# Float32 products in units, HGRN corners with 32-column weights, and a changed order of projections in a planned one-core encoder layer

## The chip, the cores and the metric

The kernel runs on one core of one Trainium2 chip. The metric is device time in microseconds of one execution; "the time" is the median of several. A profiled execution has its own time, and a span from its first instruction to its last. The engines are named as in the profile: PE is TensorE's matmuls and PEld its weight loads, DVE is VectorE, ACT is ScalarE, POOL is GpSimd, SP is SyncE, which issues the DMAs.

## The reference

One layer is applied to two sequences, a prompt of 512 tokens and a sample of 1024 tokens, with a model width of 1024:

```python
h = rms_norm(x, n_pre_mix)
proj = h @ w_in            # split: qkv, z, a, b, q_h, f_h, i_h, g_h, gate_raw
# bidirectional gated delta rule, 4 heads of 128, chunks; q, k, v behind a 5-tap conv and silu
o_a = gated_delta_chunked(q, k, v, g[0], beta[0]) + flip_seq(gated_delta_chunked(...flipped...))
y_a = (rms_norm(o_a, gdn_norm_w) * silu(z_g)) @ w_br_gdn
# bidirectional HGRN2, 4 heads of 128: f = lb + (1 - lb) * sigmoid(f_h), k = 1 - f
o_b = gla_chunked(qh, kh[0], ih, logf[0]) + flip_seq(gla_chunked(...flipped...))
y_b = (rms_norm(o_b, hg_norm_w) * silu(g_h)) @ w_br_hg
merged = gates[:, :, 0] * y_a + gates[:, :, 1] * y_b
x = x + rms_norm(merged @ w_out, n_post_mix)
h2 = rms_norm(x, n_pre_ffn)
ff = (silu(h2 @ w_gate) * (h2 @ w_up)) @ w_down
return x + rms_norm(ff, n_post_ffn)
```

Everything is float32. The chunked forms above are one way to compute the two recurrences; the kernel uses chunks of 128 tokens.

## The kernel before, in words

**Two kinds of matmul.** The large products (projections, branches, the dense part) split each float32 operand into a high and a low part in a reduced format (F32R) and add three matmuls (`mm3`). Each moves 512 columns over 128x128 weights, and a projection of 128 output columns over one block of 512 tokens is 8 x 3 = 24 of them. Its weights are loaded by one DMA (`in_w`, `get_w`) and split by ScalarE (`AF.Copy`) and VectorE (a subtraction). The small products of the mixer are float32 itself: 128x128x128 in the recurrences and for Gram matrices, transpositions against an identity, and products on 64x64, 32x32 or 128x32 parts of the array. In the trace a float32 product is two matmul records, and a transposition is one.

**The order of work is written by a program.** The function `layer` doesn't issue instructions. It records them on a `Tape`, in an order that `Plan.run` makes from five streams (`gdn_stream`, `hg_stream`, `pre_stream`, `dense_stream`, `p2_stream`). Each stream yields where it waits, for a time or for marks of other streams (`need`, `pl.mark`). Among the streams that are ready the first in the list goes on. Then `Tape.schedule` places the recorded instructions with a model of costs (`cost`: `occ` is how long the engine is taken, `dur` how long the result takes). It looks up to `AHEAD` = 500 instructions past the oldest one that hasn't been placed, and takes, on the engine that is free first, the ready instruction that stands earliest in the record. What comes out is one fixed list per engine.

**Forms and units.** A product whose weights aren't 128x128 has a `form` (rows, columns of its weights). `units` puts neighbouring products of one form, with no other matmul in between in the record, no dependence among them by way of another engine, and at most two fresh banks of PSUM, in one unit. A unit is placed as a whole, when all that its members wait for is there. The model adds `SWITCH` = 400 ns when the form changes. Float32 products with 128x128 weights and transpositions have no form before: each is placed alone, between F32R matmuls as it comes.

**HGRN corners** (`hg_attn`). Per head and block of 512 tokens, the attention inside chunks of 128 tokens is put together from levels. The 64-level, the corners of each chunk, is a product of `l64` with itself for each direction `d` and chunk `t`: 128 columns of weights, of which 64 rows of the result are needed, by 64 columns. Then come 48 products with 32-column weights, the diagonal blocks (`e2`, `e1`) and the 32-level (`l32`), each on one of four column strips of the array.

**GDN recurrence** (`gdn_mix`). Per head and chunk of 128 tokens, both directions take a step: a product with the state (`pks`), one with the inverse's factor (`pr_`), one for the new state (`pu`), with VectorE operations between, and two for the output (`po`).

**The dense list** (`dense`, `dense_stream`). For each head, projections are listed with what they wait for: z, q, i, the two forget gates f, and g. For the first sequence z and g wait for the HGRN output of the head before (`zk`), and q, i, f for that of two heads before (`hk`). `pick` takes the first item of this list if what it waits for is there, else the first open one of the 16 projections of output gates (`gates`), some of which are held back until a head's inverse or end.

**The norm of the second sequence** (`pre_stream`, `prelude`) begins when `("gin", 0)` is marked, in the last head of the first sequence, behind its inverse. It loads rows of `x_sample`, scales them, transposes them on TensorE and splits them. Its second block waits for the end of the first sequence's dense list.

Of the kernel before, what the change touches and what calls it, by code (L numbers as in the profile page):

```python
# [20 lines left out]
P = 128  # L21
# [18 lines left out]
WBUFS = (2, 2, 2)  # L40
HOLD = ((3, 2, 1, 2), (2, 2, 2, 2))
MSTEP = (24, 28)
CPOS = 3
QSQ = P * EPS ** 0.5
EPSQ = P * EPS * EPS
# [2 lines left out]
class Op:  # L48

    __slots__ = ("idx", "eng", "meth", "args", "kw", "occ", "dur", "tiles", "need", "succ", "rel", "prio", "form", "unit",  # L50
                 "asked", "port")


class VT:
# [100 lines left out]
class Tape:  # L155
# [5 lines left out]
    TAIL = {"ACT": 95, "DVE": 75, "POOL": 40}  # L161
    LANES = 8
    SWITCH = 400
    AHEAD = 500
    RATE = 260.0
    SLACK = {"sync": 600, "vector": 100, "scalar": 100, "gpsimd": 100, "tensor": 100}
# [12 lines left out]
    def __init__(self, nc):  # L179
        self.nc = nc  # L180
        self.fake = bacc.Bacc("TRN2", target_bir_lowering=False, num_devices=1)
        for n in self.ENGS:
            setattr(self, n, Tape.Eng(self, n))
        self.ops = []
        self.vts = {}
        self.pools = {}
        self.masks = {}
        self.cuts = {}
        self.count = 0

    def cut(self, name):

# [67 lines left out]
    def cost(self, o, out, ins, scal):  # L260
        e, m = o.eng, o.meth
        n = self.free_size(out)

        def psum(a):
            v = self.vts.get(a.tensor.name)
            return v is not None and v.pool.kind == "PSUM"
        if m == "dma_start":
            vo = self.vts.get(out.tensor.name)
            run = self.row(out, ins[0])
            rows = out.shape[0] * n // run  # L270
            o.form = rows * max(run * 4, 512) / self.RATE
            if vo is None or vo.pool.kind == "DRAM":
                o.dur = 1200.0
            elif [x for x in ins[0].ap if x[0] == 0 and x[1] > 1]:
                o.dur = 4000.0
            else:
                o.dur = 2000.0
            o.occ = 380.0 if rows < 512 else 450.0
            if o.dur < 2000.0 and run < P:
                o.occ = 600.0  # L280
            return
        if e == "tensor":
            if m == "transpose":
                o.occ = 110
            else:
                k = self.free_size(ins[1])
                form = (ins[0].shape[0], self.free_size(ins[0]))
                if ins[1].dtype == F32R:
                    o.occ = k / 2.4 + 13.5
                else:  # L290
                    o.occ = 2 * (2 * k / 2.4 + 5.5) if k > 32 else 24
                    if form != (P, P):
                        o.form = form
                        if form == (64, 64):
                            o.occ = 62
            o.dur = o.occ + 165
            return
        if e == "scalar":
            d = 200 + 0.84 * self.free_size(ins[0]) - (45 if psum(ins[0]) else 0) + 92 * len(scal)
            o.dur, o.occ = d, d - (95 if o.kw.get("accum_out") is None else 0)  # L300
            return
        if e == "vector":
            ps = psum(out) or any(psum(i) for i in ins)
            if not ps and m != "memset" and (m != "tensor_scalar" or n > 1):
                o.port = 138 + 65 * len(scal)
            if m == "tensor_tensor_scan":
                d = 155 + 1.98 * n
            elif m in ("tensor_copy", "tensor_scalar", "memset") and not ps:
                d = 145 + 0.53 * n
            else:  # L310
                d = 145 + 1.055 * n
            if m in ("copy_predicated", "transpose"):
                d += 30
            d += 65 * len(scal)
            o.dur, o.occ = d, d - 75
            return
        if m == "memset":
            d = 90 + 0.86 * n
        elif m == "affine_select":
            d = 100 + 1.05 * n  # L320
        else:
            d = 192 + (1.87 if n < TB else 2.15) * n
        if m != "memset":
            o.port = 138
        o.dur, o.occ = d, d - 40

    def add(self, eng, meth, args, kw):
        o = Op()
        o.idx = o.prio = len(self.ops)
        o.eng, o.meth, o.args, o.kw = eng, meth, args, kw  # L330
        o.form, o.unit, o.port = None, [o], 0
        out = args[0]
        ins = [a for a in args[1:] if isinstance(a, bass.AP)]
        scal = []
# [49 lines left out]
    def units(self):  # L384


        cur, taint, fresh = None, set(), set()
        for o in self.ops:
            if o.eng == "tensor" and o.form is not None:
                new = {v for v in o.tiles if v.pool.kind == "PSUM" and v.ops[0] is o}  # L390
                if cur and cur[0].form == o.form and not any(j in taint for j in o.need) and len(fresh | new) <= 2:
                    cur.append(o)
                    o.unit = cur
                else:
                    cur, taint, fresh = [o], set(), set()
                    o.unit = cur
                fresh |= new
            elif o.eng == "tensor":
                cur = None
            elif cur and any(j in taint or self.ops[j].unit is cur for j in o.need):  # L400
                taint.add(o.idx)

    def schedule(self):
# [77 lines left out]
        while done < len(ops):  # L481
# [18 lines left out]
            while fu and fu[0][0] <= t:  # L500
                i = heapq.heappop(fu)[1]
                heapq.heappush(re_, (ops[i].prio, i))
            o = ops[heapq.heappop(re_)[1]]
            w = t
            for x in o.unit:
                for v in x.tiles:
# [12 lines left out]
                lanes.append(t + o.dur)  # L519
            if e == "tensor":  # L520
                if o.form is not None and o.form != form:
                    t += self.SWITCH
                form = o.form
            if o.port:
                w = max(0.0, held["gpsimd" if e == "vector" else "vector"] - t - o.port)
# [186 lines left out]
def layer(ctx, tc, x_p, x_s, w_in, conv_w, a_log, dt_bias, gdn_w, lb_logits, hg_w, w_bg, w_bh,  # L712
# [631 lines left out]
    def gdn_mix(q, h, gi):  # L1344
# [125 lines left out]
        zn = []  # L1470
        for step in range(nt):
            pos, rrs = [], []
            for d in range(2):
                tg = step if d == 0 else nt - 1 - step
                b, t = divmod(tg, 4)
                tsl = slice(t * P, (t + 1) * P)
                pos.append((d, tg, b, t, tsl))
                if step == 0:
                    rrs.append(vtok[b][:, tsl])
                else:  # L1480
                    rr = sblk("rr")
                    pks = px()
                    mm(pks[:, 0:P], kT[b][:, tsl], st[d])
                    stt(rr, pks[:, 0:P], q.nec[:, tg, d, h:h + 1], vtok[b][:, tsl], ALU.mult, ALU.add)
                    rrs.append(rr)
            if step:
                yield None
            raws, vks = [], []
            for d, tg, b, t, tsl in pos:
                pr_ = px()  # L1490
                mm(pr_[:, 0:P], ws[b, d][:, t, :], rrs[d])
                if step < nt - 1:
                    vk = sblk("vk")
                    ts(vk, pr_[:, 0:P], vcs[b, d][:, t:t + 1], ALU.mult)
                    vks.append(vk)
                raw_ = sblk("raw_")
                copy(raw_, pr_[:, 0:P])
                raws.append(raw_)
            yield None
            new = {}  # L1500
            for d, tg, b, t, tsl in pos:
                if step < nt - 1:
                    pu = px()
# [4 lines left out]
                    else:  # L1508
                        stt(sn, st[d], ers[b, d][:, t:t + 1], pu[:, 0:P], ALU.mult, ALU.add)
                    new[d] = sn  # L1510
            for d, tg, b, t, tsl in pos:
                if step % 4 == 0:
                    po[d] = px()
                if step > 0:
                    mm(po[d][:, tsl], st[d], qd[b, d][:, tsl], True, False)
                mm(po[d][:, tsl], raws[d], at[b, d][:, tsl], step == 0, True)
            st = new
            for d, tg, b, t, tsl in pos:
                if step % 4 == 3:
# [3 lines left out]
                    else:  # L1523
                        tt(oT[b], oT[b], po[d], ALU.add)
                        zn.append(b)
            yield None
        yield need(("z", q.si, h))
        for b in zn:
            yield from out_norm(q, oT[b], g_gdn, q.z["z", h][b], h, b, gi["q2"][b])

    def dense(q):
        for h in range(HEADS):
# [33 lines left out]
            zk = hgk(h - 1)  # L1566
            hk = hgk(h - 1 if q.si else h - 2)
            dep = ("h", q.si, 0)
            yield (zk, dep, ("gdn", 0, 3) if q.si else dep), C_Z + h * P, zcb(("z", h)), ("z", q.si, h)
            yield (hk, dep), C_QH + h * P, cbq, None  # L1570
            yield (hk, dep), C_IH + h * P, cbv, None
            yield (hk, dep), C_FH + h * P, cbf(0), None
            yield (hk, dep), C_FH + 512 + h * P, cbf(1), ("hgin", q.si, h)
            yield (zk, ("gdn", q.si, h) if q.si else dep), C_GH + h * P, zcb(("G", h)), ("G", q.si, h)

    def gates(q):
# [57 lines left out]
    def hg_attn(q, h):  # L1634
        out = q.hg[h]
        for b in range(q.nb):
# [4 lines left out]
            pav, pbv = t4(pa), pb[:, 0:P].rearrange("p (t c) -> p t c", c=32)  # L1641
            halves = [slice(0, 64), slice(64, P)]
            yield pl.at(parts[0]["l64"], parts[1]["l64"], parts[0]["l32"], parts[1]["l32"])
            for d in range(2):
                dl = t4(parts[d]["l64"])
                for t in range(4):
                    mm(pav[:, t, halves[1 - d]], dl[:, t, :], dl[:, t, halves[1 - d]])
            for d in range(2):
                e1, e2, l32 = [parts[d][n] for n in ("e1", "e2", "l32")]
                for t in range(4):  # L1650
# [350 lines left out]

    def pre_stream():
        yield from prelude(seqs[0])
        yield need(("gin", 0))
        yield from prelude(seqs[1])

    def gdn_stream():
# [321 lines left out]
```

## Time and profile before

| what | value |
|---|---|
| median of 3 runs | 2482.34 us (2479.26 to 2483.96) |
| profiled execution, its own time | 2481.04 us |
| its span | 2479.3 us |
| mean granted TensorE clock | 0.995 |
| busy PE, PEld | 2437.4 us (98%), 2018.0 us (81%) |
| busy DVE, ACT, POOL | 1708.0 us (69%), 1276.8 us (51%), 730.7 us (29%) |
| matmul records | 13968 |
| moved by DMA | 330.37 MB, mean 133 GB/s |

The mixer takes the first half of the span, up to about 1200 us; the branches, the output projection and the dense part take the rest. Busy time of PE counts from a matmul's start to its modelled end, and matmuls overlap, so the distance from one start to the next is the better price of one. Every emitted instruction has the line of `emit`, 596, so the profile tells them apart by tiles and shapes. The tiles are large areas: `ha_a` holds the normed inputs, `wa_a` the split weights, `la_a`, `ba_a` and `sm_a` the mixer's blocks, `sa_a` constants such as the identity, and `bank` is PSUM.

### The profile page before, as it was taken

The page shows a single profiled execution, that of the slowest core. Times are in us where ns is not written, and L with a number is a line of the kernel's source. Part 1 is how long each engine was busy: PE and PEld are TensorE (multiplying, and loading weights), DVE is VectorE, ACT ScalarE, POOL GpSimd, SP SyncE. Part 2 cuts the span into 40 slices and gives each one's busy share as a digit, 9 for nine tenths or more (in the row PEclk, how much of TensorE's full clock was granted, in tenths as well). Part 3 has the DMA queues.
Part 4 walks back from the last instruction along what each step waited for, and adds up shares of the span by engine and source line. Part 5 has one row for each costly group of instructions (what it writes and reads, how often), then busy time and mean ns, then how long its engine had stood idle before and what let it go on. Part 6 is the DMA issues. An engine that isn't in the chain of part 4 may idle for free. (4 is left out here: it accounts for less than half of the span.)

```text
span 2479.3 us, 37545 instructions
## 1 busy us (share of the span) xinstructions
PE 2437.4 (98%) x13968; PEld 2018.0 (81%) x13968; DVE 1708.0 (69%) x2843; ACT 1276.8 (51%) x2166; POOL 730.7 (29%) x1011
## 2 busy tenths in 40 slices
PE   7999999999999999999999999999999999999998
PEld 6878887888888888888888888788888888888886
DVE  6868779758867677677747754664788777635458
ACT  5756667646646646546544543543444434433342
POOL 1541504141333232321000002123567675200014
PEclk9999999999999999999999999999999999999999
DMA  6234453322340330332747624544355455584463
GB/s 163 75 87 128 105 148 98 108 51 62 90 103 31 94 95 30 92 93 68 265 155 272 217 84 128 157 147 125 126 178 183 157 181 169 183 274 133 153 205 114
DMA packets 387302, 330.37 MB, mean 133 GB/s; under 512 B 55241, under 2 KB 315935, under 8 KB 387119
## 3 DMA queue, kind: packets, MB, share of 16 engines
q1 hardware_dynamic: 387119, 327.97, 43.5%
q8 instruction: 110, 1.80, 0.3%
q14 instruction: 73, 0.60, 0.1%
HBM read 251.44 MB, written 76.46 MB: 132 GB/s over the span
## 5 line engine op out<-in xcount | busy, mean ns | idle before, releaser
L596 PE MATMUL bank<-ha_a,wa_a 128*128 128x512 f32 x5496 | 1452.4, 404 | 5.8 <-ACT ha_a L596 2.3
L596 PEld LDWEIGHTS bank<-ha_a,wa_a 128*128 128x128 f32 x5496 | 1005.2, 189 | 194.2 <-DVE wa_a L596 7.6
L596 PE MATMUL bank<-xr_a,ha_a 128*128 128x512 f32 x1200 | 319.3, 395 | 0.0
L596 PE MATMUL bank<-xr_a 128*128 128x512 f32 x1386 | 315.2, 389 | 0.0
L596 PEld LDWEIGHTS bank<-xr_a 128*128 128x128 f32 x1386 | 260.1, 188 | 54.1
L596 PEld LDWEIGHTS bank<-xr_a,ha_a 128*128 128x128 f32 x1200 | 225.4, 188 | 53.9
L596 POOL TENSOR_TENSOR ba_a<-ba_a 128x512 f32<-128x512 f32 (+1 forms) x125 | 176.7, 1420 | 241.2 <-DVE ba_a L596 94.3
L596 ACT ACTIVATE la_a<-la_a 128x512 f32<-128x512 f32 (+1 forms) x335 | 209.6, 644 | 55.8 <-DVE la_a L596 42.0
L596 DVE TENSOR_TENSOR wa_a<-la_a,wa_a 128x1024 fp32r<-128x1024 f32 (+1 forms) x140 | 161.9, 1167 | 93.3 <-PE bank L596 68.9
L596 ACT ACTIVATE wa_a<-la_a 128x1024 fp32r<-128x1024 f32 (+1 forms) x140 | 136.3, 982 | 130.5 <-PE bank L596 125.3
L596 ACT ACTIVATE wa_a<-ba_a 128x1024 fp32r<-128x1024 f32 (+1 forms) x106 | 99.6, 950 | 137.8 <-PE bank L596 117.9
L596 DVE TENSOR_TENSOR wa_a<-ba_a,wa_a 128x1024 fp32r<-128x1024 f32 (+1 forms) x106 | 119.8, 1135 | 56.8 <-PE bank L596 43.1
L596 ACT ACTIVATE ha_a<-ba_a 128x512 fp32r<-128x512 f32 x130 | 81.3, 629 | 142.7 <-PE bank L596 95.4
L596 PE MATMUL bank<-ha_a 128*128 128x512 f32 x480 | 149.4, 392 | 0.0
L596 DVE TENSOR_TENSOR ha_a<-ba_a,ha_a 128x512 fp32r<-128x512 f32 x130 | 125.5, 968 | 18.9 <-ACT ha_a L596 18.6
L596 PE MATMUL bank<-wa_a,ha_a 128*128 128x512 f32 x576 | 134.1, 390 | 1.6 <-DVE wa_a L596 1.6
L596 DVE TENSOR_TENSOR la_a<-la_a 128x512 f32<-128x512 f32 (+2 forms) x184 | 125.0, 693 | 10.4 <-ACT la_a L596 9.6
L596 PEld LDWEIGHTS bank<-wa_a,ha_a 128*128 128x128 f32 x576 | 108.0, 188 | 24.5 <-DVE wa_a L596 2.0
L596 DVE TENSOR_TENSOR xr_a<-da_a,xr_a 128x1024 fp32r<-128x1024 f32 (+2 forms) x66 | 76.7, 1174 | 68.2 <-ACT xr_a L596 46.1
L596 ACT ACTIVATE xr_a<-da_a 128x1024 fp32r<-128x1024 f32 (+2 forms) x66 | 64.5, 993 | 114.7 <-PE bank L596 114.1
L596 PEld LDWEIGHTS bank<-la_a 128*32 128x32 f32 (+3 forms) x1836 | 102.5, 130 | 20.0 <-issue 4.6
L596 PE MATMUL bank<-la_a 128*32 128x32 f32 (+4 forms) x1836 | 107.7, 216 | 2.0 <-DVE la_a L596 1.6
(192 smaller groups left out, 3452.2 us busy)
## 6 DMA issues: line engine op xcount, KB each, us to landing
la_a<-w_in SPq DMA_DIRECT2D x77, 512.0 KB
ba_a<-w_ffn_up SPq DMA_DIRECT2D x37, 512.0 KB
ba_a<-w_ffn_gate SPq DMA_DIRECT2D x35, 512.0 KB
dram_a_sc<-xa_a SPq DMA_DIRECT2D x65, 256.0 KB
ba_a<-w_ffn_down SPq DMA_DIRECT2D x28, 512.0 KB
da_a<-dram_a_sc SPq DMA_DIRECT2D x28, 512.0 KB
ba_a<-w_in SPq DMA_DIRECT2D x27, 512.0 KB
dram_t_sc<-ba_a SPq DMA_DIRECT2D x20, 512.0 KB
```

What stands on the lines that cost most here:

```text
L596: f(*[m(a) for a in o.args], **{k: m(a) for k, a in o.kw.items()})
```

## The change

There are four edits.

1. Float32 products with 128x128 weights and transpositions get a form too, `FULL`. Units of this form have at most `GROUP` = 4 members, of one `part`, with one fresh bank (two where `pairs` is set, which `PAIR` and `PO`, both False, don't). `gdn_mix` starts a new part at each stage of a step. The model adds `ENTER` = 55 ns for going over to this form, and once in it TensorE takes a ready unit of this form whose place in the record is within `NEAR` = 300 of the first ready one.
2. The corners are computed in strips of 32 columns of weights: sixteen products instead of eight, only the 64 needed rows. They are recorded ahead of the 48 others as before, and have the same form (128, 32) now. The model takes 32 ns for one.
3. In the first sequence, z of heads 1 to 3 is listed behind the forget gates.
4. The norm of the second sequence waits for the end of head 1's GDN of the first sequence, `("gdn", 0, 1)`, instead of `("gin", 0)`. In the record this mark comes before the old one.

```diff
+    def apart(self, pairs=False):
+        self.part = (self.part[0] + 1, pairs)
...
             if m == "transpose":
                 o.occ = 110
+                o.form = self.FULL
...
-                    if form != (P, P):
-                        o.form = form
-                        if form == (64, 64):
-                            o.occ = 62
+                    o.form = form
+                    if form == (64, 64):
+                        o.occ = 62
+                    elif form == (P, 32) and k > 32:
+                        o.occ = 32
...
-                if cur and cur[0].form == o.form and not any(j in taint for j in o.need) and len(fresh | new) <= 2:
+                if (cur and cur[0].form == o.form and not any(j in taint for j in o.need) and len(fresh | new) <= (1 if o.form == self.FULL and not o.part[1] else 2)
+                        and (o.form != self.FULL or len(cur) < self.GROUP and o.part == cur[0].part)):
...
-            o = ops[heapq.heappop(re_)[1]]
+            k = None
+            if e == "tensor" and form == self.FULL:
+                k = min((x for x in re_ if ops[x[1]].form == form and x[0] < re_[0][0] + self.NEAR), default=None)
+            if k is None:
+                k = heapq.heappop(re_)
+            else:
+                re_.remove(k)
+                heapq.heapify(re_)
+            o = ops[k[1]]
...
-                    t += self.SWITCH
+                    t += self.ENTER if o.form == self.FULL else self.SWITCH
...
-            yield (zk, dep, ("gdn", 0, 3) if q.si else dep), C_Z + h * P, zcb(("z", h)), ("z", q.si, h)
+            if not (h and q.si == 0):
+                yield (zk, dep, ("gdn", 0, 3) if q.si else dep), C_Z + h * P, zcb(("z", h)), ("z", q.si, h)
             yield (hk, dep), C_QH + h * P, cbq, None
             yield (hk, dep), C_IH + h * P, cbv, None
             yield (hk, dep), C_FH + h * P, cbf(0), None
             yield (hk, dep), C_FH + 512 + h * P, cbf(1), ("hgin", q.si, h)
+            if h and q.si == 0:
+                yield (zk, dep), C_Z + h * P, zcb(("z", h)), ("z", q.si, h)
...
-            for d in range(2):
-                dl = t4(parts[d]["l64"])
-                for t in range(4):
-                    mm(pav[:, t, halves[1 - d]], dl[:, t, :], dl[:, t, halves[1 - d]])
+            for t in range(4):
+                for j in range(4):
+                    d, sl = j // 2, slice(32 * j, 32 * j + 32)
+                    dl = t4(parts[d]["l64"])
+                    mm(pav[sl, t, halves[1 - d]], dl[:, t, sl], dl[:, t, halves[1 - d]])
...
-        yield need(("gin", 0))
+        yield need(("gdn", 0, 1))
         yield from prelude(seqs[1])
```

The lines left out are the new constants, the `part` that each instruction is given, and the five calls of `apart` in `gdn_mix`: ahead of `pks`, of `pr_`, of `pu`, of `po`, and at the step's end.

More of the change, by code (lines that the diff above doesn't have):

```diff
@@ L42 @@
 MSTEP = (24, 28)
+PAIR = False
+PO = False
 CPOS = 3
@@ L50 @@
     __slots__ = ("idx", "eng", "meth", "args", "kw", "occ", "dur", "tiles", "need", "succ", "rel", "prio", "form", "unit",
-                 "asked", "port")
+                 "asked", "port", "part")
 class VT:
@@ L163 @@
     SWITCH = 400
+    FULL = (P, P)
+    ENTER = 55
+    NEAR = 300
+    GROUP = 4
     AHEAD = 500
@@ L189, in __init__ @@
         self.count = 0
+        self.part = (0, False)
+    def apart(self, pairs=False):
+        self.part = (self.part[0] + 1, pairs)
     def cut(self, name):
@@ L330, in add @@
         o.eng, o.meth, o.args, o.kw = eng, meth, args, kw
-        o.form, o.unit, o.port = None, [o], 0
+        o.form, o.unit, o.port, o.part = None, [o], 0, self.part
         out = args[0]
@@ L1472, in gdn_mix @@
             pos, rrs = [], []
+            nc.apart(PAIR)
             for d in range(2):
@@ L1488, in gdn_mix @@
             raws, vks = [], []
+            nc.apart(PAIR)
             for d, tg, b, t, tsl in pos:
@@ L1500, in gdn_mix @@
             new = {}
+            nc.apart(PAIR)
             for d, tg, b, t, tsl in pos:
@@ L1510, in gdn_mix @@
                     new[d] = sn
+            nc.apart(PO)
             for d, tg, b, t, tsl in pos:
@@ L1526, in gdn_mix @@
             yield None
+            nc.apart()
         yield need(("z", q.si, h))
```

## The prediction

> **What bounds the kernel now.** I read the page first (span, busy shares, clock slices), then busy time by stretch, then TensorE's own order of time at the places that the change touches, then the DMA queue's order.
>
> ```profile
> span 2479.3 us, 37545 instructions
> PE 2437.4 (98%) x13968; PEld 2018.0 (81%) x13968; DVE 1708.0 (69%) x2843; ACT 1276.8 (51%) x2166; POOL 730.7 (29%) x1011
> ...
> 124.00:192.00 68.00, 60.98 (x408) 48.65 (x407) 43.94 (x84) 35.22 (x59) 30.61 (x97) 0.92 0.44 106
> 200.00:300.00 100.00, 99.99 (x707) 83.78 (x706) 78.24 (x146) 68.36 (x114) 38.35 (x86) 1.00 0.41 104
> 410.00:425.00 15.00, 13.65 (x146) 10.62 (x144) 14.76 (x34) 8.63 (x20) 0.80 (x4) 1.00 0.20 55
> ```
>
> The stretches give length, then busy time (instructions) of TensorE's matmuls, its weight loads, VectorE, ScalarE and GpSimd, then the granted clock. TensorE has work in 98% of the span, and in a stretch of the mixer such as 200 to 300 us in all of it. So whatever shortens TensorE's own list of work there shortens the run; whatever merely makes another engine faster does not. There is one real hole behind the prologue: between 124 and 192 us TensorE is idle for 68.00 - 60.98 = 7.0 us, and its mean clock is 0.92, another 68 x 0.08 = 5.4 us lost. Together 12.4 us are to be had there and no more.
>
> **Corners with 32-column weights.** Per head and block of 512 tokens, eight products of 128-column weights and 64 columns are replaced by sixteen of 32-column weights and 64 columns. There are 12 such blocks (4 heads, 3 blocks): 96 products go, 192 come. In the trace each float32 product is two records. First block, then a later one:
>
> ```profile
> 111.72 3.80 PE L596 MATMUL bank<-ha_a,wa_a 128*128 128x512 f32 x16
> 115.36 0.33 PE L596 MATMUL bank<-la_a 128*128 128x64 f32 x2
> 115.50 0.48 PE L596 MATMUL bank<-ha_a,wa_a 128*128 128x512 f32 x1
> 115.81 0.33 PE L596 MATMUL bank<-la_a 128*128 128x64 f32 x2
> ...
> 120.30 0.72 PE L596 MATMUL bank<-ha_a,wa_a 128*128 128x512 f32 x2
> 120.94 1.21 PE L596 MATMUL bank<-la_a 128*32 128x32 f32 x96
> 122.08 2.35 PE L596 MATMUL bank<-ha_a,wa_a 128*128 128x512 f32 x9
> ...
> 850.19 0.33 PE L596 MATMUL bank<-la_a 128*128 128x64 f32 x2
> 850.36 0.28 PE L596 MATMUL bank<-sa_a,la_a 128*128 128x128 f32 x1
> 850.39 0.72 PE L596 MATMUL bank<-ha_a,wa_a 128*128 128x512 f32 x2
> 850.95 0.33 PE L596 MATMUL bank<-la_a 128*128 128x64 f32 x2
> ```
>
> Starts are what counts, since durations overlap. Sixteen projection matmuls (128x512) from 111.72 to 115.36 us: 0.2275 us each. A corner product between two of them: from 115.36 to 115.81 us less one projection matmul = 0.22 us. Beside a transposition (the single record): 850.19 to 850.95 less two projection matmuls = 0.305, and a transposition is one record of 128 columns, half of the 0.226 us that such a product takes below, so 0.19. I take 0.20: 96 x 0.20 = 19.2 us go.
>
> What comes has no row of its own. Lower end: the 32-column records beside which it will stand, 96 in 1.14 us (120.94 to 122.08) = 0.012 per record; 192 x 2 x 0.012 = 4.6 us. Upper end: a 64-column record alone, two in 0.14 us (115.36 to 115.50) = 0.07; 26.9 us, as if the four column strips did not work side by side. Nearest row: 64x64 products, 64 columns too, two blocks of the array at a time:
>
> ```profile
> 212.15 0.68 PE L596 MATMUL bank<-ba_a,la_a 64*64 64x64 f32 x16
> 212.76 1.66 PE L596 MATMUL bank<-ha_a,wa_a 128*128 128x512 f32 x6
> ```
>
> Sixteen records in 0.61 us = 0.038; with four strips instead of two, half of it, 0.019: 384 x 0.019 = 7.3 us. Net of this part **-11.9 us**; ends -14.6 and +7.7. Nothing is added for entering the other form: 120.30 to 120.94 us is 0.64 for two projection matmuls, so entering costs 0.185 us, it is paid once per block now, and the corners come into the same unit. That unit grows from 1.14 to about 1.75 us, in which no other product can go ahead.
>
> [...]
>
> **Float32 products as units.** Up to four neighbouring float32 products or transpositions that write one bank go out together, and the planner books 55 ns for changing over from a projection matmul. What does changing over cost?
>
> ```profile
> 1066.18 0.61 PE L596 MATMUL bank<-la_a,ba_a 128*128 128x128 f32 x4
> 1066.63 0.39 PE L596 MATMUL bank<-ba_a 128*128 128x128 f32 x2
> 1066.85 0.39 PE L596 MATMUL bank<-la_a 128*128 128x128 f32 x2
> 1066.99 0.71 PE L596 MATMUL bank<-ha_a,wa_a 128*128 128x512 f32 x2
> 1067.54 0.38 PE L596 MATMUL bank<-la_a 128*128 128x128 f32 x2
> 1067.68 0.47 PE L596 MATMUL bank<-ha_a,wa_a 128*128 128x512 f32 x1
> 1067.99 0.38 PE L596 MATMUL bank<-ba_a 128*128 128x128 f32 x2
> ```
>
> From 1066.18 to 1067.54 us stand four products in a row (eight records) and two projection matmuls: (1.36 - 0.455) / 4 = 0.226 each. Alone, 1067.54 to 1067.99: 0.45 - 0.2275 = 0.2225. Changing over costs nothing that these rows can show (they are rounded to 0.01 us). The groups by form hold 1950 such records in ten rows, of which these are the first and the last:
>
> ```profile
> L596 PE MATMUL bank<-sm_a,la_a 128*128 128x128 f32 x350 | 64.7, 274 | 0.0
> ...
> L596 PE MATMUL bank<-ba_a,la_a 128*128 128x128 f32 x100 | 18.8, 274 | 0.0
> ```
>
> At most 975 products x 0.005 us = 5 us either way; I take **0**. What the part does change is order: a unit waits for the inputs of all its members, and holds TensorE for up to 4 x 0.226 = 0.9 us. In the recurrence the two outputs' four products become one unit, so the older two wait for the younger's inputs; nobody but the block's output reads them. A product of the recurrence's chain that falls behind such a unit waits up to 3 x 0.226 = 0.68 us longer than behind a single one. Projection matmuls cover that while there are some; a price without that cover stands below as a rival.
>
> **Forget gates ahead of z, the second norm at another mark.** In the first sequence, z of heads 1 to 3 waits for the HGRN output of the head before, and everything behind z in the list waits with it. With z behind, q, i and both forget gates of head 1 are open as soon as head 0's list is through. That is what lacks in the hole:
>
> ```profile
> 85.31 0.63 SPq L596 DMA_DIRECT2D la_a<-w_in  x1
> ...
> 112.17 0.39 SPq L596 DMA_DIRECT2D ba_a<-w_in  x1
> ...
> 140.69 0.43 SPq L596 DMA_DIRECT2D la_a<-w_in  x1
> ...
> 354.28 0.86 SPq L596 DMA_DIRECT2D ba_a<-x_sample  x2
> ```
>
> The queue loads one projection's weights between 85.9 and 140 us; nothing is left to project. Four more projections are 4 x 24 x 0.2275 = 21.8 us of TensorE, three times the 7.0 us of idle time. Each also brings a load of 0.4 us on a queue that is mostly idle there, a split on ScalarE and VectorE and an activation chain:
>
> ```profile
> L596 DVE TENSOR_TENSOR wa_a<-la_a,wa_a 128x1024 fp32r<-128x1024 f32 x116 | 144.9, 1258 | 88.2 <-PE bank L596 67.1 <-ACT wa_a L596 18.0 <-issue 2.6
> L596 ACT ACTIVATE la_a<-la_a 128x512 f32<-128x512 f32 x322 | 195.8, 627 | 51.1 <-DVE la_a L596 37.8 <-POOL la_a L596 5.4 <-DMA la_a<-dram_cr_sc 2.5
> ```
>
> Between 124 and 192 us VectorE has 68.00 - 43.94 = 24 us free against 4 x 1.26 = 5.0 for the splits, and ScalarE 33 us against some ten activations of 0.63 and its own half of each split, 1024 columns, at most twice 0.63. It fits. The half clock comes with the idle time and should go with it. I take **-9 us** of the 12.4: stalls in merge steps, where TensorE waits for VectorE's copy of its own result, aren't all covered by work that runs as soon as it can. Ends 0 and -12.4.
>
> The same 21.8 us are missing later in the first sequence, whose total is unchanged. There the new mark helps: the second sequence's norm now waits for the end of head 1, which comes earlier in the stream than the old mark, which is set behind head 3's inverse (its input rows were loaded from 354 us). So its gates are open when the first list ends. z itself waits for the same HGRN output as before and is next in the list then, so the output norm that reads it is not later. The moved norm's loads, squares and 64 transpositions are the same in number; they go past weight loads on SyncE's queue and land on VectorE at 78% (200 to 300 us), where there is room. **0**.
>
> **Sum.** The profiled execution took 2481.0 us (span 2479.3 and 1.7 around it), 1.3 under the median of 2482.3. 2481.0 - 11.9 - 0 - 9 = **2460 us**.
>
> **Rivals.**
> (a) The hole moves. The work that fills 124 to 192 us is missing at the end of the first sequence, where TensorE is already 1.35 us idle between 410 and 425 us. If the 9 us return there, 2481.0 - 11.9 = 2469 us. For it: the heads' chain (inverse on GpSimd, merges, recurrence) sets a least time per head. Against it: the earlier norm, and no idle time between 200 and 300.
> (b) The column strips do not overlap: +7.7 in place of -11.9, with the -9 2480 us, no change. Against it: a 64-column record alone takes 0.07 us, so one of 32 columns would take some 0.035, and the row has 0.012.
> (c) Slower: the units delay the recurrence. Of its 48 steps (4 heads, 4 + 8), each can wait 0.68 us longer, 33 us when all of it is bare; with the two gains of 20.9 us that decides against the change from 63% of that on, 2481 - 20.9 + 33 = 2493 us at worst. For it: the steps are a chain of single products. Against it: at 200 to 300 us TensorE is never idle, so a late chain is covered.
> (d) The hole closes altogether and corners cost the lower end: -14.6 - 12.4, 2454 us.
>
> **How the numbers follow.** Forecast, with (d) as its upper side, 0.62; (a) 0.18; (b) 0.08; (c) 0.07; a schedule that comes out otherwise at no net change 0.05. The likeliest gives 2460. Its range: with +-3 for changing over and the ends of the other terms, 2450 to 2467. To leave out no more than 2 in 10, the range takes in (a) with its own spread: 2446 to 2474. Runs of this kernel lie 4.7 us apart, so 0.2% (5 us) is about what can be told from no change. Faster: the forecast, (a) and a part of (b), 0.82; same 0.10; slower 0.08.
>
> **What would show it.** After: no 128x64 record with 128-column weights, 384 with 32-column ones, in one run with the 96, the whole run near 1.75 us and below 2.0; between 124 and 192 us TensorE busy above 66 of 68 us and clock 1.00; x_sample loaded well before 354 us; 400 to 500 us as full as before. Wrong corners show as runs above 2.5 us, (a) as idle time between 300 and 500 us, (c) as idle time spread over the recurrences with the 0.226 us of a product unchanged.
>
> [...]

## The result, and the profile after

The changed kernel takes 2461.14 us (median of 4, 2460.43 to 2462.66), the one before in the same rounds 2482.38 us (2479.26 to 2483.96): ratio 0.9918, 95% interval 0.9902 to 0.9934, 21.2 us less. The two profiled executions stand at 2462.66 and 2481.04 us; the first part of what follows accounts for these 18.4 us. Every emitted instruction now has line 619 in place of 596.

The head of the page of the changed kernel:

```profile
span 2460.9 us, 37970 instructions
PE 2420.2 (98%) x14160; PEld 2005.9 (82%) x14160; DVE 1704.7 (69%) x2843; ACT 1276.9 (52%) x2166; POOL 743.7 (30%) x1011
```

Span less busy PE is 41.9 us before and 40.7 us after. TensorE is idle almost as long as it was; its busy time fell by 17.2 us. Where that time stood is read from busy time by stretch. First the changed kernel (columns as in the prediction):

```profile
0.00:30.00 30.00, 13.76 (x45) 10.28 (x46) 19.26 (x72) 20.23 (x48) 9.77 (x33) 1.00 0.90 242
124.00:192.00 68.00, 67.22 (x581) 56.93 (x580) 49.63 (x95) 39.59 (x68) 24.64 (x56) 1.00 0.41 102
192.00:300.00 108.00, 102.93 (x746) 83.40 (x745) 96.19 (x202) 79.81 (x155) 55.92 (x114) 1.00 0.59 158
236.00:284.00 48.00, 43.14 (x391) 34.34 (x391) 46.81 (x109) 33.18 (x69) 14.21 (x29) 1.00 0.53 145
410.00:425.00 15.00, 15.00 (x68) 12.43 (x67) 11.53 (x24) 13.71 (x27) 10.16 (x22) 1.00 0.23 67
600.00:1200.00 600.00, 596.00 (x4678) 504.96 (x4678) 443.55 (x847) 359.94 (x624) 172.89 (x298) 1.00 0.31 88
```

The same view of the kernel before, for the stretches that the prediction doesn't show:

```profile
0.00:30.00 30.00, 16.45 (x60) 12.38 (x61) 19.32 (x72) 19.80 (x48) 9.87 (x33) 0.89 0.92 245
192.00:300.00 108.00, 107.99 (x742) 90.27 (x741) 83.19 (x154) 72.45 (x119) 40.26 (x90) 1.00 0.44 113
236.00:284.00 48.00, 48.00 (x342) 40.66 (x341) 34.19 (x55) 32.79 (x53) 17.70 (x40) 1.00 0.55 141
600.00:1200.00 600.00, 596.91 (x4416) 505.99 (x4415) 442.80 (x838) 355.83 (x622) 172.38 (x304) 1.00 0.30 82
```

| stretch, us | idle TensorE before | after |
|---|---|---|
| 0 to 30 | 13.6, clock 0.89 | 16.2, clock 1.00 by the record |
| 124 to 192 | 7.0, and 5.4 by the clock | 0.8, clock 1.00 |
| 192 to 300 | 0.0 | 5.1 |
| 600 to 1200 | 3.1 | 4.0 |

The hole between 124 and 192 us is closed: 11.6 of its 12.4 us. A new one stands between 192 and 300 us, with VectorE busy for 46.81 of the 48 us from 236 to 284, against 34.19 before. And the prologue leaves TensorE idle 2.7 us longer. The stretches from 300 to 600 us and from 1200 to 1700 us together lost 3.3 us of idle time.

The clock of the prologue can't be compared by these records. First the kernel before, then the changed one:

```profile
24.00:27.00 3.00, 3.00 (x8) 2.32 (x7) 1.50 (x6) 0.00 (x0) 0.00 (x0) 0.50 1.19 290
```

```profile
27.00:30.00 3.00, 3.00 (x8) 2.36 (x8) 0.00 (x0) 0.00 (x0) 0.86 (x1) 1.00 1.17 291
```

In both, projection matmuls start 0.43 us apart (seven starts from 24.08 to 26.64 us before, five from 28.00 to 29.71 us after) against 0.2275 at a clock of 1.00 (111.72 to 115.36 us before), but only the first row has a clock of 0.50 beside it. In the second the half clock seems to be missing from the record, so no gain is counted for the prologue's clock.

That new hole comes with the second sequence's norm, as the run with the old mark shows below. From the changed kernel's timeline of the DMA queue, its first load (at 354.28 us before):

```profile
198.00 2.45 SPq L619 DMA_DIRECT2D ba_a<-x_sample  x2
```

The corners, in TensorE's order of time in the changed kernel:

```profile
657.76 0.25 PE L619 MATMUL bank<-la_a 128*32 128x64 f32 x2
657.78 0.25 PE L619 MATMUL bank<-ba_a 128*32 128x64 f32 x2
...
658.23 0.68 PE L619 MATMUL bank<-la_a 128*32 128x32 f32 x48
...
659.42 0.50 PE L619 MATMUL bank<-ha_a,wa_a 128*128 128x512 f32 x1
```

Thirty-two records of 64 columns start within 0.47 us (657.76 to 658.23), 0.015 us each. The groups by form have all 384 of them:

```profile
L619 PE MATMUL bank<-la_a 128*32 128x64 f32 x240 | 6.5, 222 | 0.0
...
L619 PE MATMUL bank<-ba_a 128*32 128x64 f32 x144 | 4.5, 222 | 0.0
```

So 384 x 0.015 = 5.8 us came. Against the 19.2 us that were forecast to go, that would be 13.4 us off TensorE's list. In the run with the corners alone (below) busy time falls by less, from 2437.4 to 2425.5 us:

```profile
PE 2425.5 (98%) x14160; PEld 2003.9 (81%) x14160; DVE 1709.9 (69%) x2843; ACT 1277.1 (52%) x2166; POOL 733.6 (30%) x1011
```

These 11.9 us and the clock's 5.4 make 17.3, which is the fall of busy time, 17.2 us. Idle time fell by 1.2: 6.2 in the hole at 124 to 192 us, against 5.1 more elsewhere. That is the account of the 18.4 us.

### The profile page after: what moved, and what is told of

It is laid out like the page before. It is cut to its first block, busy times and chain, and to the rows that moved or that the text cites. A ratio compares the mean times of both kernels' runs of the same rounds, so it can differ in the third digit from the quotient of the medians.

```text
span 2460.9 us, 37970 instructions
## 1 busy us (share of the span) xinstructions
PE 2420.2 (98%) x14160; PEld 2005.9 (82%) x14160; DVE 1704.7 (69%) x2843; ACT 1276.9 (52%) x2166; POOL 743.7 (30%) x1011
## 4 chain that ended last, share of the span: by engine, by line
PE 82%; DVE 5%; issue 1%; DMA 1%; ACT 1%; POOL 0%; SPq 0%; DVEq 0%; POOLq 0%; ACTq 0%
PE bank L619 82%; DVE la_a L619 2%; DVE ba_a L619 1%; DVE wa_a L619 1%; DVE sm_a L619 1%; ACT ba_a L619 0%; ACT la_a L619 0%; DMA la_a<-w_in 0%; DMA dram_a_sc<-ba_a 0%; DMA ba_a<-dram_u_sc 0%; SPq L619 0%; DVE ha_a L619 0%; DMA dram_g_sc<-ba_a 0%; POOL ba_a L619 0%; ACT wa_a L619 0%
## 5 line engine op out<-in xcount | busy, mean ns | idle before, releaser
L619 PE MATMUL bank<-ha_a,wa_a 128*128 128x512 f32 x5496 | 1342.3, 395 | 3.8 <-DVE wa_a L619 1.7
L619 PEld LDWEIGHTS bank<-ha_a,wa_a 128*128 128x128 f32 x5496 | 1015.5, 188 | 213.4 <-DVE wa_a L619 8.4
L619 POOL TENSOR_TENSOR ba_a<-ba_a 128x512 f32<-128x512 f32 (+1 forms) x137 | 183.4, 1345 | 250.2 <-DVE ba_a L619 84.7
L619 POOL TENSOR_TENSOR la_a<-la_a 128x256 f32<-128x256 f32 (+1 forms) x54 | 56.3, 1056 | 450.5 <-DVE la_a L619 411.9
L619 DVE TENSOR_TENSOR wa_a<-ba_a,wa_a 128x1024 fp32r<-128x1024 f32 (+1 forms) x110 | 125.7, 1150 | 52.2 <-PE bank L619 38.9
L619 DVE TENSOR_TENSOR la_a<-la_a 128x512 f32<-128x512 f32 (+3 forms) x192 | 130.0, 689 | 8.3 <-ACT la_a L619 7.4
L619 POOL TENSOR_TENSOR la_a<-la_a,sm_a 128x30 f32<-128x30 f32 (+40 forms) x217 | 110.2, 508 | 16.0
```

The costliest lines, as they stand in the source:

```text
L619: f(*[m(a) for a in o.args], **{k: m(a) for k, a in o.kw.items()})
```

## The experiments

"Changed" is the changed kernel. Ratios are to the kernel before on the same chip (2482.51, 2482.25 and 2481.57 us in the three groups), with the 95% interval. Differences to Changed are to 2461.14 us, and in the third group, where Changed ran again on the same chip, to 2461.19. In the second group it wasn't run; the three medians of the kernel before lie 0.9 us apart, so differences there are good to about 1 us.

### First group: the parts alone

**Corners alone** (the kernel before with this edit):

```diff
+            for t in range(4):
+                for j in range(4):
+                    d, sl = j // 2, slice(32 * j, 32 * j + 32)
+                    dl = t4(parts[d]["l64"])
+                    mm(pav[sl, t, halves[1 - d]], dl[:, t, sl], dl[:, t, halves[1 - d]])
```

and the model's 32 ns for one.

> The kernel before with the corners' edit alone (sixteen strips of 32-column weights, and the model's 32 ns for one). Theory (the parts add up; TensorE's list of work is what counts): the corners take 13.4 us off the list (19.2 us before, 32 records in 0.48 us per block after, 5.8 us in all), so the run is 11 to 15 us shorter than the kernel before, the hole between 124 and 192 us stays (idle 6 to 8 us). Rival (the corners ran in time that was free anyway, the gain is the order of work): less than 4 us shorter.

Measured 2476.2 us, 0.9973 (0.9963 to 0.9984): 6.3 us less, between the theory's 11 to 15 and the rival's 4. The profiled execution is 5.5 us shorter: 11.9 us of busy time are gone, and 6.4 came back as idle time (41.9 to 48.3 us). Most of that stands in the stretch of the second sequence's mixer:

```profile
600.00:1200.00 600.00, 592.38 (x4642) 498.31 (x4642) 441.04 (x834) 358.07 (x623) 173.64 (x298) 1.00 0.31 86
```

7.6 us idle here against 3.1 before; another 1.7 us stand between 124 and 192 us (8.7 idle, where the theory had 6 to 8). A shorter list is not a shorter run by as much.

**z behind the forget gates, old mark** (the kernel before with this edit):

```diff
-            yield (zk, dep, ("gdn", 0, 3) if q.si else dep), C_Z + h * P, zcb(("z", h)), ("z", q.si, h)
+            if not (h and q.si == 0):
+                yield (zk, dep, ("gdn", 0, 3) if q.si else dep), C_Z + h * P, zcb(("z", h)), ("z", q.si, h)
...
+            if h and q.si == 0:
+                yield (zk, dep), C_Z + h * P, zcb(("z", h)), ("z", q.si, h)
```

> The kernel before with z of heads 1 to 3 listed behind the forget gates, the second norm at its old mark. Theory (four more projections fill the hole, but VectorE then gets the moved norm): without the moved norm there is no new hole between 200 and 300 us, idle time between 124 and 192 us under 2 us at clock 1.00; the run is 8 to 12 us shorter. Rival (a hole that moves): what is filled early is missing at the first sequence's end, TensorE idle 5 us and more between 300 and 500 us, and the run is within 4 us of the kernel before.

Measured 2473.43 us, 0.9963 (0.995 to 0.9977): 9.1 us less, as the theory has it. By stretch:

```profile
124.00:192.00 68.00, 67.90 (x564) 57.92 (x563) 51.23 (x96) 41.11 (x70) 23.26 (x52) 1.00 0.47 119
192.00:300.00 108.00, 107.13 (x744) 90.05 (x743) 82.99 (x147) 70.34 (x115) 46.72 (x108) 1.00 0.47 116
390.00:410.00 20.00, 14.62 (x65) 10.75 (x64) 17.93 (x51) 13.34 (x34) 10.18 (x24) 0.83 0.16 41
```

This edit alone closes the hole, and leaves 192 to 300 us full. What is missing instead is at 390 to 410 us: 5.4 us idle and a clock of 0.83. The dense list has run out and TensorE waits for the norm, whose split is `ha_a`. From the waits between 380 and 410 us:

```profile
PE bank L596 <- ACT ha_a L596: 3.1, 1, 3.1
```

**z and the mark** (the edit above, and the second one):

```diff
-        yield need(("gin", 0))
+        yield need(("gdn", 0, 1))
```

> The kernel before with both changes of order, z behind the forget gates and the second norm at the end of head 1. Theory (the moved norm loads VectorE between 200 and 300 us): VectorE busy above 92 of the 108 us from 192 to 300, TensorE idle about 5 us there, the run 4 to 7 us shorter than the kernel before and some 4 us longer than the one with z alone. Rival (the hole moves): the earlier norm is what keeps the first sequence's end full, so this run is the shorter one of the two, by 4 us or more.

Measured 2482.84 us, 1.0001 (0.9992 to 1.001): with the mark added all 9 us are lost again. The theory had the stretch right and the time wrong. By stretch:

```profile
192.00:300.00 108.00, 100.24 (x712) 83.07 (x711) 91.39 (x194) 74.83 (x148) 49.65 (x109) 0.97 0.56 147
390.00:410.00 20.00, 20.00 (x110) 16.74 (x109) 13.95 (x21) 12.17 (x19) 16.98 (x41) 1.00 0.08 18
1200.00:1700.00 500.00, 492.75 (x2271) 405.28 (x2263) 296.62 (x472) 223.28 (x364) 42.48 (x38) 0.99 0.54 170
```

It removes the hole at 390 us (5.4 us idle and 3.4 of clock) and makes one of 7.8 us, with 3.2 of clock in it, between 192 and 300 us. Together that is only some 1.3 us worse than z alone. Most of the loss stands elsewhere, in the last row above. With z alone that stretch reads:

```profile
1200.00:1700.00 500.00, 497.44 (x2257) 409.97 (x2256) 295.75 (x466) 223.60 (x364) 48.50 (x43) 1.00 0.54 171
```

That is 4.7 us of idle time more, and some 5 of clock, long after the moved norm. Why it comes is not shown. This profiled execution (2486.59 us) is among the longest of a kernel whose eleven runs lie 7.8 us apart, so the median may have less of it.

**Units alone** (Changed, with corners, z and the mark as before: the three diffs above in reverse).

> The changed kernel without the corners' edit, with z in its old place and the norm at its old mark: units of float32 products alone. Theory (changing over costs nothing, units hold up the first transpositions): the first projection matmul starts 3 to 5 us later than in the kernel before, and the run is 0 to 4 us longer. Rival (entering costs something for each of some 800 groups of float32 products, a third as many with units): the run is 4 us or more shorter.

Measured 2480.66 us, 0.9994 (0.9985 to 1.0003). Alone the units can't be told from nothing. But the profile has the first projection matmul later. First this kernel, then the kernel before:

```profile
24.72 5.75 PE L619 MATMUL bank<-ha_a,wa_a 128*128 128x512 f32 x12 [1.44 <-ACT ha_a L619]
```

```profile
20.67 1.22 PE L596 MATMUL bank<-ha_a,wa_a 128*128 128x512 f32 x2 [2.13 <-ACT ha_a L596]
```

### Second group: from the changed kernel

**Old mark** (Changed with `need(("gin", 0))`).

> The changed kernel with the second norm back at its old mark, behind head 3's inverse. Theory (two places, two causes: at the new mark the norm fills VectorE between 236 and 284 us, at the old mark the dense list runs out and TensorE waits for the norm's split): TensorE idle under 1.5 us between 192 and 300 us, 4 us and more between 360 and 420 us, there waiting for ha_a; the run within 4 us of the changed kernel. Rival (the new mark costs its 9 us with units too, as it did without): the run is 6 to 10 us shorter than the changed kernel. Second rival (with units the new mark is what brings the gain): 6 us or more longer.

Measured 2468.74 us, 0.9941 (0.9928 to 0.9953), 7.6 longer than Changed. By stretch:

```profile
192.00:300.00 108.00, 107.54 (x764) 89.55 (x763) 84.07 (x151) 72.70 (x119) 49.02 (x108) 1.00 0.53 134
360.00:420.00 60.00, 54.67 (x368) 42.51 (x366) 50.81 (x119) 47.34 (x110) 28.81 (x67) 0.97 0.55 160
```

The theory had the places right: the hole at 192 to 300 us goes, and one of 5.3 us opens at 360 to 420, of which one wait of 2.2 us is for `ha_a`. Another 3.0 us of idle time stand between 300 and 360. It had the size wrong; the time is on the second rival's side. The same mark that costs 9 us without units and corners gains 7.6 with them; since most of those 9 us don't stand where the norm was moved, neither number is the mark's own worth.

**Strips in turn** (Changed):

```diff
-            for t in range(4):
-                for j in range(4):
+            for j in range(4):
+                for t in range(4):
```

> The changed kernel with the two loops of the corners exchanged, so that four products follow each other on one column strip before the next strip's turn; the same products, the same count. Theory (64-column records are cheap because four strips work side by side): 32 records take 1.5 to 2.2 us instead of 0.48, the run is 12 to 20 us longer than the changed kernel. Rival (a 32-column weight load and its record are cheap by themselves, strips do not matter): 32 records stay under 0.7 us, the run is within 3 us.

Measured 2468.62 us, 0.9945 (0.9933 to 0.9958), 7.5 longer than Changed. In TensorE's order of time:

```profile
619.87 0.72 PE L619 MATMUL bank<-ba_a 128*32 128x64 f32 x13
620.37 0.24 PE L619 MATMUL bank<-la_a 128*32 128x64 f32 x1
...
622.15 0.50 PE L619 MATMUL bank<-ha_a,wa_a 128*128 128x512 f32 x1
```

With four products (eight records) in a row on one strip, 13 records take 0.50 us: 0.038 each against 0.015 in turn over four strips. From the first corner to the next projection matmul it is 2.28 us against 1.66 above; 12 x 0.62 = 7.4 us, the whole difference, and TensorE's busy time rose as much (2420.2 to 2427.5 us). It is less than was expected because the later records mix in with those of another strip (0.028 us each from 620.42 to 620.56 us) and with 32-column ones. So the strips do work side by side, by the 0.015 us against 0.038, and rival (b) is out. Whether it is the weight loads or the matmuls that overlap, this run doesn't separate.

**Mark one head later** (Changed with `need(("gdn", 0, 2))`).

> The changed kernel with the second norm at the end of head 2 instead of head 1, between the two marks. Theory (the norm needs a place where VectorE has room and the dense list isn't empty yet): neither hole, TensorE idle under 2 us in each of 192 to 300 and 300 to 420 us, the run 3 to 7 us shorter than the changed kernel. Rival (the chain of heads sets a least time and the hole only moves): one stretch of 50 us between 200 and 450 us still has 4 us of idle time, the run within 2 us of the changed kernel.

Measured 2458.16 us, 0.9904 (0.989 to 0.9917), 3 us under Changed, not told apart by the intervals. Between 192 and 300 us 0.9 us of idle time is left; between 300 and 420 it is 2.6, more than the 2 that were expected at most. By stretch:

```profile
192.00:300.00 108.00, 107.11 (x761) 89.07 (x760) 83.62 (x150) 73.37 (x123) 48.61 (x108) 1.00 0.52 140
300.00:420.00 120.00, 117.38 (x828) 97.73 (x827) 107.28 (x234) 88.69 (x182) 52.38 (x109) 1.00 0.36 99
```

**Prologue's transpositions single** (Changed; in the norm's function, for the first sequence):

```diff
             for k in range(4):
+                if share:
+                    nc.apart()
                 tr(pt[:, k, :], xs[i][:, k * P:(k + 1) * P])
```

> The changed kernel with each transposition of the first sequence's norm in a part of its own, so that none of them waits for a unit. Theory (units hold up the first transpositions): the first projection matmul starts at 20 to 22 us as in the kernel before instead of at 25 us, the run is 2 to 4 us shorter than the changed kernel. Rival (VectorE's order of work in the prologue is what is late, and that comes from the model's 55 ns and the order, not from waiting for a unit): the first projection matmul still starts at 24 us and later.

Measured 2460.04 us, 0.9911 (0.9898 to 0.9925), 1.1 less than Changed: not resolved. The late start itself was due to the units of four transpositions, since all but 0.5 us of it is gone:

```profile
21.21 0.73 PE L619 MATMUL bank<-ha_a,wa_a 128*128 128x512 f32 x2 [1.45 <-ACT ha_a L619]
```

In Changed the same line reads:

```profile
25.01 5.28 PE L619 MATMUL bank<-ha_a,wa_a 128*128 128x512 f32 x11 [1.44 <-ACT ha_a L619]
```

### Third group: parts in company

**Changed again.**

> The changed kernel itself, on the same chip as the three others, as their measure. Every theory: 2458 to 2464 us.

Measured 2461.19 us, 0.9916 (0.9903 to 0.993). By stretch, for the comparison with the run without units:

```profile
192.00:300.00 108.00, 103.03 (x746) 83.53 (x745) 96.59 (x201) 79.95 (x156) 55.97 (x115) 1.00 0.59 158
600.00:1200.00 600.00, 596.53 (x4687) 505.93 (x4687) 443.55 (x846) 359.18 (x622) 173.88 (x298) 1.00 0.31 89
```

**Corners, z and mark without units** (the kernel before with the three diffs of the first group).

> The kernel before with the corners' edit, z behind the forget gates and the second norm at the end of head 1: everything but the units of 128x128 products. Theory (the parts add up): the corners alone were 6 us shorter, the two changes of order together 0, so 2474 to 2478 us, and the units are what brings the rest, 13 to 17 us. Rival (the parts do not add up, since each schedule falls out some us better or worse by itself): 2463 to 2470 us, as the corners' 13 us of work are gone with any order.

Measured 2475.73 us, 0.9979 (0.997 to 0.9988). By stretch:

```profile
192.00:300.00 108.00, 99.41 (x713) 81.92 (x713) 96.21 (x199) 72.89 (x144) 60.75 (x131) 0.94 0.51 138
600.00:1200.00 600.00, 592.11 (x4644) 498.04 (x4643) 443.09 (x837) 359.13 (x624) 171.79 (x298) 1.00 0.30 84
```

The theory holds: corners and the two changes of order add up (-6.3 and +0.3 us alone, -5.8 together), and in this company the units bring 14.5 us, against 1.9 us alone. The two profiled executions differ by more, 18.4 us. By the rows: 3.6 us of idle time and 108 x 0.06 = 6.5 us of clock between 192 and 300 us, and 4.4 us of idle time between 600 and 1200. Another 3.8 us of idle time stand between 1200 and 1700.

**55 to 50 ns** (Changed with `ENTER = 50`).

> The changed kernel with 50 ns instead of 55 in the planner's model for going over to a 128x128 float32 product; no instruction differs, only their order. Theory (the order is set by dependences and the record): within 2 us of the changed kernel. Rival (the planner's list is so sensitive that any change moves the time by some us, and single parts under 5 us can't be told from that): 3 us or more away, either way.

Measured 2467.25 us, 0.9941 (0.9928 to 0.9953), 6.1 longer: the rival holds. Five nanoseconds in the planner's model, which change no instruction, give another list and a larger hole, 8.2 us idle against 5.0:

```profile
192.00:300.00 108.00, 99.80 (x731) 82.16 (x730) 91.29 (x195) 77.54 (x153) 52.45 (x116) 0.98 0.56 154
```

So a difference of some 6 us between two lists doesn't tell what an edit is worth in itself. One such change was tried; how far others would move the time is not known.

**Mark one head later and single transpositions together.**

> The changed kernel with the first sequence's transpositions each in a part of its own and the second norm at the end of head 2. Theory (the two holes are separate and each mend keeps its worth): first projection matmul before 22 us, TensorE idle under 1.5 us between 192 and 300 us, the run 3 to 7 us shorter than the changed kernel. Rival (what is mended early comes back later, as the end of the first sequence takes its time anyway): within 2 us of the changed kernel.

Measured **2453.28 us**, 0.9886 (0.9873 to 0.99), 7.9 under Changed on the same chip, somewhat more than expected. It beats both kernels. The first projection matmul starts at 20.13 us. By stretch:

```profile
192.00:300.00 108.00, 107.97 (x767) 90.36 (x766) 84.58 (x152) 74.30 (x127) 50.88 (x111) 1.00 0.48 132
236.00:284.00 48.00, 47.97 (x300) 41.23 (x301) 37.53 (x73) 32.44 (x57) 14.29 (x32) 1.00 0.54 141
300.00:420.00 120.00, 119.56 (x917) 98.92 (x917) 110.97 (x244) 89.49 (x182) 48.61 (x107) 1.00 0.37 104
```

VectorE has 37.53 us to do where Changed has 46.81, and TensorE is full there and behind it.

## Why the prediction was right, point by point

The forecast lies 1.1 us under the median (2460 against 2461.14) and 2.7 under the profiled execution. The two gains of its sum, corners and hole, are found in the profile. That the sum fits so well is luck in part: it adds up terms as if each were worth the same alone and in company. Alone, the corners (-6.3 us), both changes of order (+0.3) and the units (-1.9) come to 7.9 of the 21.2 us. The other 13 us come only with all of them, and the sum has no term for that. (The range's lower end, 2446 us, isn't worked out in the prediction; nothing here hangs on it.)

1. **Corners, -11.9.** With this edit alone TensorE's busy time fell by 11.9 us. Inside the term two errors made up for each other: a record takes 0.015 us, not 0.019, so 5.8 us came instead of 7.3; then by busy time some 17.7 us went, an estimate, instead of 19.2. The run up to the next projection matmul is 1.66 us against some 1.75 forecast. That it is the four strips side by side is shown by exchanging the loops (0.038 us a record in place of 0.015). What the step left out is that a shorter list isn't filled by itself: alone this edit brought 6.3 us. The rest came back as idle time, 4.5 us of it at 600 to 1200 us and 1.7 in the old hole.
2. **Units, 0.** Right for the units alone. In company they brought 14.5 us, which the sum has nowhere, and there they removed stalls where rival (c) had them make some. What makes the size is open: a list that differs by a constant of the model moves the time by 6.1 us as well. The step also looked at the recurrence alone. The units of four hold up the prologue too, where the first projection matmul stands 4.3 us later (25.01 against 20.67), with no projection there to cover it.
3. **The hole, -9.** It closed as forecast, by 11.6 of 12.4 us, and the reason is shown by the edit of z alone: the hole went (0.1 us idle, the clock 1.00 in place of 0.92), and the run is 9.1 us shorter.
4. **The moved norm, 0.** This step failed: "land on VectorE at 78% (200 to 300 us), where there is room" took an average of a long stretch in place of the 48 us in which the norm stands. There VectorE rose from 34.19 to 46.81 us and TensorE lost 4.9 us. The step's other half was right, that the new mark helps when the first list ends: 410 to 425 us is full in Changed, and with the old mark TensorE is idle for 5.3 us between 360 and 420 us. Against the old mark the term was not 0: 7.6 us shorter with units and corners, 9.4 longer without them. Of the three marks tried in Changed, head 2 has the least idle time from 192 to 420 us (3.5 us, against 5.6 at head 1 and 8.8 at the old mark).
5. **Rival (a)** named 300 to 500 us as the place to which the hole moves; that stretch is full in Changed (410 to 425 us: 15.00 of 15). With z alone and the old mark the hole did move there in part, to 390 to 410 us. In Changed it moved in part to 192 to 300 us, by way of point 4.

So the hole's larger gain (2.6 us) and less idle time elsewhere (3.3 us) made up for most of the 5.1 us at 192 to 300 us, the 2.7 of the prologue and 0.9 at 600 to 1200. What is left is the 2.7 us between the sum and the profiled execution, to 0.1.

## What to carry to other kernels

Price small matmuls from start to start, and look at which strip the next one stands on: in turn over four strips a 64-column record cost 0.015 us here, with four products in a row on each strip 0.038. Before work is moved under other work, read the engine it lands on in the very stretch where it will stand, not its mean over a hundred microseconds. Where a planner writes the list, try each part in the company of the others and find out first how far a harmless constant moves the time; here it was 6 us.

## What the runs showed of the hardware

In the old hole half clock came without a pause longer than 1.3 us. In the kernel before, by stretch and by the waits between 124 and 154 us (total, times, longest):

```profile
124.00:154.00 30.00, 25.21 (x218) 19.43 (x217) 22.38 (x45) 14.89 (x26) 11.77 (x37) 0.83 0.42 100
```

```profile
PE bank L596 <- DVE ba_a L596: 1.8, 3, 1.0
PE bank L596 <- ACT wa_a L596: 1.6, 2, 1.3
```

That longest pause is one of the waits for `wa_a`, and the clock is 0.83 over 30 us, which is 5.1 us lost, as much as the 4.8 us of pauses. The half clock stands in one piece, 0.50 from 143.5 to 153.7 us; its start by stretch:

```profile
139.00:142.00 3.00, 1.46 (x42) 1.15 (x40) 2.79 (x6) 1.85 (x3) 0.00 (x0) 1.00 0.28 39
142.00:145.00 3.00, 2.16 (x52) 1.17 (x52) 2.92 (x8) 0.49 (x1) 0.00 (x0) 0.74 1.04 279
145.00:148.00 3.00, 2.36 (x19) 1.45 (x17) 2.27 (x6) 3.00 (x6) 0.00 (x0) 0.50 1.03 233
```

Most records of the first two rows are of 32x32 products (32 of 42, and 48 of 52). Before the clock falls, 32 such records stand between pauses of 0.26 and 1.28 us:

```profile
140.17 0.45 PE L596 MATMUL bank<-la_a 32*32 32x32 f32 x32 [0.26 <-DVE la_a L596]
141.91 0.49 PE L596 MATMUL bank<-wa_a,ra_a 128*128 128x512 f32 x1 [1.28 <-ACT wa_a L596]
```

Whether the pauses alone bring the half clock, or the small products between them have a part in it, no run here separates.

A 64-column record with 32-column weights took 0.015 us from start to start in turn over four strips (Changed, 657.76 to 658.23 us), and 0.038 us with four products in a row on each strip (strips in turn, 619.87 to 620.37 us).

After the change TensorE also pauses where nothing that the profile shows holds it, between small products:

```profile
713.20 0.21 PE L619 MATMUL bank<-la_a,ba_a 32*32 32x32 f32 x1 [1.33 <-issue]
```

There are 2.1 us of this in three places in Changed and 3.1 us in five with corners alone, none in the kernel before. Some of it may be records that the trace lacks; what it is stays open.
